# Turning the memory queries on VectorE and through DRAM in place of TensorE transposes, in a two-layer hybrid decoder

## The chip, the cores and the metric

The kernel runs on one core of one Trainium2 chip. The metric is the device time of one execution in microseconds (us); the runs of the kernel before took 383.99, 384.08 and 385.17 us, median 384.08. The profile is of one further execution, taken by the hardware profiler.

Engines are called TensorE (PE; its weight loads are PEld), VectorE (DVE), ScalarE (ACT), GpSimd (POOL) and SyncE (SP, here only an issuer of DMAs). A line such as L1259 is a line of the kernel before.

## The reference

Two layers work on `x` of 256 tokens by 1024 columns. Each normalises `x`, multiplies it by one wide input matrix, runs three branches side by side and adds the gated, projected result to `x`.

```python
for l in range(DEPTH):                                   # DEPTH = 2
    h = rms_norm(x, norm_g[l])
    proj = h @ w_in[l]                                   # 1024 x 5120
    q_a, k_a, v_a, q_h, f_h, i_h, q_m, z = jnp.split(proj, split_points, axis=-1)
    ...                                                  # o_a: causal attention, 8 heads x 64
    ...                                                  # o_h: HGRN2 recurrence, 4 heads x 128
    kv_m = rms_norm(mem, mem_norm_g[l]) @ w_mem_kv[l]    # 256 memory tokens
    k_m, v_m = jnp.split(kv_m, 2, axis=-1)
    km = rms_norm(k_m.reshape(B, M, MEM_HEADS, MEM_HEAD_DIM), mem_k_norm[l])
    qm = rms_norm(q_m.reshape(B, S, MEM_HEADS, MEM_HEAD_DIM), mem_q_norm[l])
    o_m = memory_attention(qm, km, vm).reshape(B, S, G)  # 4 heads x 128
    y = jnp.concatenate([o_a, o_h, o_m], axis=-1) * jax.nn.silu(z)
    x = x + y @ w_out[l]
```

The change is about `qm`, the queries of the memory branch: 256 tokens by 512 columns (4 heads of 128).

## The kernel before

**Weights in chunks.** All weights pass through SBUF as 60 chunks per layer, each 128 rows by 1024 columns (512 KB). SyncE loads a chunk into `wr` (4 buffers), ScalarE casts it to a rounded high half `wh` (3 buffers, line 213), and VectorE subtracts to get the low half `wl` (3 buffers, line 227). A product is three matmuls: high by high, high by low, low by high. Chunk numbers below count from a layer's start: 0 to 7 memory keys and values, 8 to 15 the HGRN forget and query gates, 16 to 19 keys, 20 to 23 HGRN input, 24 to 27 queries, 28 to 31 HGRN gate, 32 to 35 memory queries, 36 to 39 values, 40 to 43 and 44 to 47 the two other gates, 48 to 59 the output projection. A chunk of the values is 12 matmuls of 512 columns on PE (lines 292 to 294); a chunk of the gates is eight of 512 columns with `wh` and then eight of 256 columns with `wl` (line 275).

**Side work.** All else of the branches is written as generators that are stepped between the matmul groups. A scheduler sets the order of each engine's instructions; where it is not left to it, `in_turn` chains (functions `order_of_attention`, `order_of_memory`) write the order out by hand: which `wl` stands ahead of which piece of VectorE's side work, and the same for ScalarE. Engines and queues work strictly in their order, so a piece that waits holds all that stands behind it.

**The memory queries.** `g_qm` (line 1241) copies the two PSUM results to `qm` on ScalarE, takes the sums of squares, and then turns `qm` so that the head dimension lies on the partitions: for each half `t` of the tokens, four TensorE transposes of 128x128 into a PSUM tile (line 1259), a ScalarE cast to the high half `qmh` (line 1261) and a VectorE subtraction to the low half `qml` (line 1262). That makes 8 transposes per layer and 16 in all. They are placed among the values' matmuls. `g_mem_unit` then multiplies `qmh` and `qml` with the turned keys (`kmh`, `kml`; 24 score matmuls of 256 columns per layer, printed as line 275 `sd<-kml,qmh` and so on), takes row maxima (`mxm`), a scaled negative maximum (`nbm`), exponentials on ScalarE (line 1300) and the rest of the softmax.

**The other way to turn a tile.** `across` (line 88) is used for keys, queries, the HGRN output and the attention weights P: VectorE transposes 32x32 blocks into a tile `blk` (line 95), one DMA writes it to DRAM (`there`, line 106), and four DMAs read it back in the turned order, 32 partitions each (line 111). The default queue is SyncE's; with `q=nc.gpsimd` all five DMAs are on GpSimd's. The tile `blk` is one buffer, unless `stage` names the tag of another.

## Time and profile before

| | |
|---|---|
| median of the runs (range) | 384.08 us (383.99 to 385.17) |
| the profiled execution | 383.72 us, span 381.9 us |
| PE busy | 376.4 us, 99% of the span |
| PEld busy | 317.1 us, 83% |
| VectorE busy | 322.4 us, 84% |
| ScalarE busy | 250.5 us, 66% |
| GpSimd busy | 112.3 us, 29% |
| granted PE clock | 0.999 of full speed |
| DMA | 87.64 MB, mean 229 GB/s |
| stretch 129 to 135 us (scores of layer 0) | VectorE busy 6.00 of 6.00 us, DMA share 0.85 |

The span is the time from the first to the last instruction of the profiled execution. In a timeline a row has the start, the time from the first start to the last end of the merged instructions, engine, line, operation, output tile <- input tiles, and a count; a bracket tells how long the engine was idle ahead of it and what released it. Matmuls are pipelined, so their rows overlap and the distance of two starts tells more than a duration. The last rows of an answer on one tile give the time from a DMA's issue to its landing.

### The profile page before, as it was taken

The numbers are of one execution on the slowest core, as the hardware profiler recorded it, in microseconds if no ns is written. First come the engines' busy times: TensorE is split into PE (matmuls) and PEld (weight loads), VectorE is DVE, ScalarE is ACT, GpSimd is POOL, SyncE is SP. The second block draws the span as 40 slices with busy tenths as digits, with TensorE's granted clock in tenths as the row PEclk, the third lists the DMA queues.
The fourth block names the chain that finished last, engine by engine and source line by source line (L and its number), as shares of the span: only waits on it lengthen the run. The fifth ranks groups of instructions, "written<-read, shape, count | busy, mean of one in ns | idle before, by whom it ended". The sixth has DMA issues, their size and how long they took to land.

```text
span 381.9 us, 6807 instructions
## 1 busy us (share of the span) xinstructions
PE 376.4 (99%) x2431; PEld 317.1 (83%) x2431; DVE 322.4 (84%) x596; ACT 250.5 (66%) x428; POOL 112.3 (29%) x199
## 2 busy tenths in 40 slices
PE   8999999999999999999999999999999999999996
PEld 5888888878887898888888888888888888888885
DVE  4789978999769999967597889899897799998573
ACT  5988866439669839664367857455665993894540
POOL 3176889500700722220021030030052042225000
PEclk9999999999999999999999999999999999999999
DMA  8986695377823889896459667736876168989712
GB/s 267 419 321 190 235 288 172 118 269 232 295 82 128 269 274 355 307 270 214 167 175 317 189 203 233 257 125 232 257 223 222 55 246 266 348 262 307 224 57 110
DMA packets 27250, 87.64 MB, mean 229 GB/s; under 512 B 3792, under 2 KB 6224, under 8 KB 27216
## 3 DMA queue, kind: packets, MB, share of 16 engines
q1 hardware_dynamic: 22304, 71.31, 55.0%
q0 software_dynamic: 4624, 15.73, 13.8%
q8 instruction: 19, 0.31, 0.3%
q10 hardware_dynamic: 288, 0.15, 0.1%
q14 instruction: 15, 0.12, 0.1%
HBM read 76.18 MB, written 11.01 MB: 228 GB/s over the span
## 4 chain that ended last, share of the span: by engine, by line
PE 76%; POOL 7%; DVE 7%; DMA 3%; issue 3%; ACT 2%; DVEq 0%; ACTq 0%
PE acc L275 19%; PE acc L1438 17%; PE acc L312 12%; PE acc L293 7%; PE acc L292 6%; PE acc L294 6%; PE sd L275 4%; PE sd L279 3%; DVE wl L227 2%; DMA qT<-there 1%; POOL rt L605 1%; POOL rt L606 1%; DMA there<-blk 1%; ACT P L1169 1%; POOL mk L653 1%
## 5 line engine op out<-in xcount | busy, mean ns | idle before, releaser
L227 DVE TENSOR_TENSOR wl<-wr,wh 128x1024 fp32r<-128x1024 f32 x96 | 116.7, 1219 | 17.7 <-ACT wh L213 17.5
L213 ACT CAST wh<-wr 128x1024 fp32r<-128x1024 f32 x96 | 100.9, 1053 | 46.0 <-PE acc L275 18.4
L293 PE MATMUL acc<-wl,hT 128*128 128x512 f32 x192 | 75.4, 393 | 0.3 <-DVE wl L227 0.3
L294 PE MATMUL acc<-wh,hT 128*128 128x512 f32 x192 | 74.8, 390 | 0.0
L292 PE MATMUL acc<-wh,hT 128*128 128x512 f32 x192 | 70.5, 395 | 0.0
L275 PE MATMUL acc<-hT,wh 128*128 128x512 f32 x256 | 64.0, 391 | 0.0
L275 PEld LDWEIGHTS acc<-hT,wh 128*128 128x128 f32 x256 | 46.4, 189 | 8.3
L292 PEld LDWEIGHTS acc<-wh,hT 128*128 128x128 f32 x192 | 35.9, 188 | 8.0 <-issue 0.7
L293 PEld LDWEIGHTS acc<-wl,hT 128*128 128x128 f32 x192 | 36.1, 188 | 7.6 <-DVE wl L227 0.5
L294 PEld LDWEIGHTS acc<-wh,hT 128*128 128x128 f32 x192 | 36.1, 188 | 7.5
L1438 PE MATMUL acc<-wl,yh 128*128 128x512 f32 (+1 forms) x96 | 37.1, 387 | 0.0
L1438 PE MATMUL acc<-wh,yl 128*128 128x512 f32 (+1 forms) x96 | 37.1, 387 | 0.0
L217 ACT ACTIVATE wh<-wr,gT 128x1024 fp32r<-128x1024 f32 (+1 forms) x29 | 28.6, 1002 | 12.4 <-DMA wr<-in_w_mem_kv_dram 4.8
L275 PEld LDWEIGHTS acc<-hT,wl 128*128 128x128 f32 x256 | 34.7, 190 | 2.2
L231 DVE SCALAR_TENSOR_TENSOR wl<-wr,gT,wh 128x1024 fp32r<-128x1024 f32 (+1 forms) x29 | 31.1, 1095 | 5.3 <-ACT wh L217 5.3
L275 PE MATMUL acc<-hT,wl 128*128 128x256 f32 x256 | 35.4, 282 | 0.0
L1438 PE MATMUL acc<-wh,yh 128*128 128x512 f32 (+1 forms) x96 | 30.6, 390 | 0.0
L106 POOL DMA_DIRECT2D there<-blk x9 | 5.8, 649 | 80.3 <-DVE hgm L699 39.8
L312 PE MATMUL acc<-wh,mTh 128*128 128x512 f32 x64 | 25.2, 396 | 0.4 <-ACT mTh L433 0.4
L312 PE MATMUL acc<-wh,mTl 128*128 128x512 f32 x64 | 24.8, 390 | 0.0
L1169 ACT ACTIVATE P<-P,nba,rq 128x128 f32<-128x128 f32 (+1 forms) x32 | 17.1, 544 | 8.0 <-DVE nba L1163 8.0
L1438 PEld LDWEIGHTS acc<-wh,yl 128*128 128x128 f32 x96 | 18.0, 188 | 3.7
(237 smaller groups left out, 648.8 us busy)
## 6 DMA issues: line engine op xcount, KB each, us to landing
wr<-in_w_in_dram SPq DMA_DIRECT2D x80, 512.0 KB, 4.4
wr<-in_w_out_dram SPq DMA_DIRECT2D x24, 512.0 KB, 7.3
wr<-in_w_mem_kv_dram SPq DMA_DIRECT2D x15, 512.0 KB, 5.2
there<-blk POOLq DMA_DIRECT2D x9, 512.0 KB, 5.0
there<-blk POOLq DMA_DIRECT2D x4, 768.0 KB, 6.2
PT<-there POOLq DMA_DIRECT2D x16, 192.0 KB, 5.8
there<-blk SPq DMA_DIRECT2D x4, 512.0 KB, 2.9
P<-there POOLq DMA_DIRECT2D x16, 128.0 KB, 7.3
```

Of the source, the lines that this page charges most:

```text
L213: N["wh", i] = nc.scalar.copy(whs[i], raws[i])
L217: N["wh", i] = nc.scalar.activation(whs[i][:, sl], raws[i][:, sl], AF.Copy, scale=gT[:, g:g + 1])
L227: N["wl", i] = nc.vector.tensor_tensor(wls[i], raws[i], whs[i].bitcast(F32), op=OP.subtract)
L231: ins = nc.vector.scalar_tensor_tensor(wls[i][:, sl], in0=raws[i][:, sl], scalar=gT[:, g:g + 1], in1=whs[i][:, sl].bitcast(F32), op0=OP.mu ...
L275: nc.tensor.matmul(o, lhsT=a, rhs=b, start=s, stop=e)
L279: ins = nc.tensor.matmul(o, lhsT=a, rhs=b, start=s, stop=e)
L292: N["mm", i, j, t] = nc.tensor.matmul(acc[t], lhsT=th[:, k, ts], rhs=wH, start=k == 0, stop=False)
L293: N["mm l", i, j, t] = nc.tensor.matmul(acc[t], lhsT=th[:, k, ts], rhs=wL, start=False, stop=False)
L294: N["mm r", i, j, t] = nc.tensor.matmul(acc[t], lhsT=tl[:, k, ts], rhs=wH, start=False, stop=k == 7)
L312: N["kv", i, g, t, j] = nc.tensor.matmul(acc[g][t], lhsT=x[:, c, ts], rhs=y, start=c == 0 and j == 0, stop=c == 7 and j == 2)
L1169: N["exp", u, c] = nc.scalar.activation(P[:, i, kc[t]], P[:, i, kc[t]], AF.Exp, bias=nb[:, c:c + 1], scale=rq[:, r:r + 1], accum_out=sm[:, ...
L1438: ins = nc.tensor.matmul(a, lhsT=y, rhs=wt[:, cs], start=n == (0 if to is None else nk - 2) and j == 0, stop=n == nk - 1 and j == 2)
```

## The change

`g_qm` no longer uses TensorE. Once the HGRN recurrence has used its input `ih` (new flag `recurred`), `qm` as a whole goes through `across`: one VectorE block transpose of 128x1024 into the space of `ih`, a write to DRAM on GpSimd's queue, and four loads back into `qm` on SyncE's queue (the new argument `back`). ScalarE then casts `qmh` and VectorE subtracts `qml` from SBUF, in the strided order that `across` leaves. In the hand-written order the block transpose stands behind `wl` 38 and ahead of the first P transpose (`turned0`), both `qml` stand ahead of `wl` 41 (before: one behind `wl` 39, one behind the HGRN output's transpose), both `qmh` stand behind the second `va` copy and ahead of `wh` 43, and the row maxima `mxm` of the scores, of which two were placed ahead of `wl` 42 and `wl` 43, are all behind `wl` 43.

```diff
-    def across(dst, src, n, stage=None, free=None, name=None, q=None, behind=None, pace=(2, 4)):
+    def across(dst, src, n, stage=None, free=None, name=None, q=None, behind=None, pace=(2, 4), back=None):
...
-            ins = q.dma_start(dst[c * 32:c * 32 + 32], there[:, :, c].rearrange("q j r -> j q r"))
+            ins = (back or q).dma_start(dst[c * 32:c * 32 + 32], there[:, :, c].rearrange("q j r -> j q r"))
...
+        done.add(f"recurred{l}")
         r = rsq("hg", ss, 8, 128)
...
-        yield 2
+        flat = qm.rearrange("p t s -> p (t s)")
+        while f"recurred{l}" not in done:
+            yield
+        yield from across(flat.rearrange("p (q r) -> p q r", q=4), flat, 8, "ih", q=nc.gpsimd, name=f"qm{l}", pace=(1, 1),
+                          back=nc.sync)
         qmh = sb.tile([128, 4, 256], F32R, name="qmh", tag="ih", bufs=1)
         qml = sb.tile([128, 4, 256], F32R, name="qml", tag="hF", bufs=1)
         for t in range(2):
-            ts = slice(t * 128, (t + 1) * 128)
-            yield from room("sd")
-            pt = side_tile()
-            for h in range(4):
-                N["qm turn", t, h] = nc.tensor.transpose(pt[:, h * 128:(h + 1) * 128], qm[:, t, h * 128:(h + 1) * 128],
-                                                         ident)
-            N["qmh", t] = nc.scalar.copy(qmh[:, :, ts], heads(pt, 4))
-            N["qml", t] = nc.vector.tensor_tensor(qml[:, :, ts], heads(pt, 4), qmh[:, :, ts].bitcast(F32), op=OP.subtract)
-            rel()
-        yield 2
+            N["qmh", t] = nc.scalar.copy(strip_of(qmh, t), strips(flat)[:, :, t])
+            N["qml", t] = nc.vector.tensor_tensor(strip_of(qml, t), strips(flat)[:, :, t],
+                                                  strip_of(qmh, t).bitcast(F32), op=OP.subtract)
+        yield
...
-        in_turn(w("wl", 37), w("wl", 38), ("across", f"turned0{l}"))
-        for h in range(4):
-            in_turn(("mm", c + 37, 1, 1), ("qm turn", 1, h))
+        in_turn(w("wl", 37), w("wl", 38), ("across", f"qm{l}"))
...
```

VectorE in layer 0, from `wl` of chunk 37 (`wl_1494`) over chunk 38 to chunk 39 (`wl_1593` before, `wl_1597` now); `P_1349` is the first P tile, `hgm` and `ssq` are small sums for the norms. Before:

```order
L227 TENSOR_TENSOR wl_1494<-wr_1359,wh_1445 128x1024
L227 TENSOR_TENSOR wl_1544<-wr_1384,wh_1492 128x1024
L95 STREAM_TRANSPOSE blk_1635<-P_1349 128x1536
L699 TENSOR_SCALAR hgm_1522<-ssh_1449 128x8
L695 TENSOR_REDUCE ssq_1550<-sq_1554 128x4
L695 TENSOR_REDUCE ssq_1550<-sq_1557 128x4
L227 TENSOR_TENSOR wl_1593<-wr_1443,wh_1542 128x1024
```

Now:

```order
L227 TENSOR_TENSOR wl_1494<-wr_1359,wh_1445 128x1024
L227 TENSOR_TENSOR wl_1544<-wr_1384,wh_1492 128x1024
L95 STREAM_TRANSPOSE blk_1566<-qm_1551 128x1024
L95 STREAM_TRANSPOSE blk_1625<-P_1349 128x1536
L699 TENSOR_SCALAR hgm_1522<-ssh_1449 128x8
L695 TENSOR_REDUCE ssq_1550<-sq_1554 128x4
L695 TENSOR_REDUCE ssq_1550<-sq_1557 128x4
L227 TENSOR_TENSOR wl_1597<-wr_1443,wh_1542 128x1024
```

The transpose of `qm` stands between `wl` 38 and the P transpose; all behind it, `wl` 39 with it, keeps its order.

TensorE in layer 0, from the last matmul of the values; `acc` are the gate group's results, `sd` those of the scores. Before:

```order
L294 MATMUL acc<-wh,hT 128x512
L275 MATMUL sd<-kml,qmh 128x256
L275 MATMUL sd<-kmh,qml 128x256
L275 MATMUL sd<-kmh,qmh 128x256
L275 MATMUL sd<-kml,qmh 128x256
L275 MATMUL sd<-kmh,qml 128x256
L275 MATMUL sd<-kmh,qmh 128x256
L275 MATMUL acc<-hT,wh 128x512 x7
```

Now:

```order
L294 MATMUL acc<-wh,hT 128x512
L275 MATMUL acc<-hT,wh 128x512 x24
L275 MATMUL acc<-hT,wl 128x256 x5
L275 MATMUL sd<-kml,qmh 128x256
L275 MATMUL acc<-hT,wl 128x256
L275 MATMUL sd<-kml,qmh 128x256 x3
L275 MATMUL acc<-hT,wl 128x256 x2
L275 MATMUL acc<-hT,wh 128x512 x6
L275 MATMUL sd<-kmh,qml 128x256
```

The first score matmul has moved behind the high-half matmuls of chunks 40 to 42 and five of the low-half ones of chunk 40; the 24 score matmuls themselves are the same.

More of the change, by code (lines that the diff above doesn't have):

```diff
@@ L1380, in order_of_attention @@
                 in_turn("score", (p, c + 34, t // 2, t % 2))
-        in_turn(w("wl", 37), w("wl", 38), ("across", f"turned0{l}"))
-        for h in range(4):
-            in_turn(("mm", c + 37, 1, 1), ("qm turn", 1, h))
+        in_turn(w("wl", 37), w("wl", 38), ("across", f"qm{l}"))
         in_turn(("last mask", 0), ("nba", 0), ("first mask", 1), ("last mask", 1), ("nba", 1), w("wl", 36), ("ria", 0),
                 *(("scale", 0, i) for i in range(5)), ("ss", "h", 0), *(("scale", 0, i) for i in range(5, 8)),
-                ("ss", "h", 1), w("wl", 37), ("across", f"turned0{l}"), ("ms", "hg"), ("ss", "qm", 0),
-                ("ss", "qm", 1), w("wl", 39), ("qml", 0), ("ms", "qm"), *(("zh", i) for i in range(8)), ("ria", 1),
-                w("wl", 40), ("across", f"zh{l}"), ("qml", 1), *(("scale", 1, i) for i in range(8)), w("wl", 41),
-                ("across", f"turned1{l}"), ("mxm", 0, 0), w("wl", 42), ("mxm", 1, 0), w("wl", 43))
+                ("ss", "h", 1), w("wl", 37), ("across", f"qm{l}"), ("across", f"turned0{l}"), ("ms", "hg"), ("ss", "qm", 0),
+                ("ss", "qm", 1), w("wl", 39), ("ms", "qm"), *(("zh", i) for i in range(8)), ("ria", 1),
+                w("wl", 40), ("across", f"zh{l}"), *(("scale", 1, i) for i in range(8)), ("qml", 0), ("qml", 1),
+                w("wl", 41), ("across", f"turned1{l}"), w("wl", 42), w("wl", 43))
         in_turn(*(("exp", 0, i) for i in range(5)), w("wh", 36), *(("exp", 0, i) for i in range(5, 8)),
                 ("sq", "h", 0), ("sq", "h", 1), w("wh", 37), ("qm", 0), ("sq", "qm", 0), w("wh", 38), ("qm", 1),
-                ("sq", "qm", 1), w("wh", 39), ("qmh", 0), *(("exp", 1, i) for i in range(8)), w("wh", 40), ("qmh", 1),
-                w("wh", 41), ("va", 0), w("wh", 42), ("va", 1), w("wh", 43))
+                ("sq", "qm", 1), w("wh", 39), *(("exp", 1, i) for i in range(8)), w("wh", 40),
+                w("wh", 41), ("va", 0), w("wh", 42), ("va", 1), ("qmh", 0), ("qmh", 1), w("wh", 43))
     def order_of_norm(l):
@@ L1415, in order_of_memory @@
         unit = lambda k, u: [(k, u, i) for i in range(4)]
-        in_turn(w("wl", 43), ("sum", A_, 0), ("mxm", 0, 1), ("mxm", 1, 1), w("wl", 44), ("sum", A_, 1), ("nbm", 0),
+        in_turn(w("wl", 43), ("mxm", 0, 0), ("mxm", 0, 1), ("sum", A_, 0), w("wl", 44), ("mxm", 1, 0), ("mxm", 1, 1), ("sum", A_, 1), ("nbm", 0),
                 w("wl", 45), ("sum", A_, 2), ("nbm", 1), w("wl", 46), ("rim", 0), *unit("scalem", 0), ("sum", A_, 3),
```

## The prediction

> **What bounds the kernel now.** I read the page first, then the timelines of TensorE (PE) and VectorE (DVE) where the transposes stand, then the DMAs' landing times.
>
> ```profile
> PE 376.4 (99%) x2431; PEld 317.1 (83%) x2431; DVE 322.4 (84%) x596; ACT 250.5 (66%) x428; POOL 112.3 (29%) x199
> ```
>
> PE is busy for 99% of the span of 381.9 us. So the kernel is one queue of matmuls: an instruction taken out of it is a gain of its own step in the queue, and a wait put into it is a loss of its length, unless something later absorbs either. The question is what PE has in the place of the 16 transposes.
>
> **What the transposes hold.** Here is PE around the eight of layer 0 (line 1259, two groups of four), down to the first matmul that needs the low half `wl` of chunk 39.
>
> ```profile
> 119.81 0.60 PE L1259 MATMUL sd<-ident,qm 128*128 128x128 f32 x4
> 120.70 0.50 PE L293 MATMUL acc<-wl,hT 128*128 128x512 f32 x1 [0.28 <-DVE wl L227]
> 121.03 0.39 PE L294 MATMUL acc<-wh,hT 128*128 128x512 f32 x1
> ...
> 122.62 0.60 PE L1259 MATMUL sd<-ident,qm 128*128 128x128 f32 x4
> 122.98 0.49 PE L293 MATMUL acc<-wl,hT 128*128 128x512 f32 x1
> 123.30 0.39 PE L294 MATMUL acc<-wh,hT 128*128 128x512 f32 x1
> ...
> 126.75 0.39 PE L293 MATMUL acc<-wl,hT 128*128 128x512 f32 x1
> 126.97 0.39 PE L294 MATMUL acc<-wh,hT 128*128 128x512 f32 x1
> ```
>
> Matmuls overlap, so the step is from start to start: 0.22 to 0.23 us for a plain one (126.75 to 126.97). From the second group's start to the second matmul behind it there are 0.68 us (122.62 to 123.30); without the transposes one plain step of 0.23 would stand there. A group holds PE for 0.45 us, not for its busy time. The first group is different. Behind it PE still waits 0.28 us for `wl` of chunk 37. With those transposes gone PE waits longer, and the matmul starts at 120.70 as before: gain 0.
>
> In layer 1 the same place, from the second matmul behind the first group:
>
> ```profile
> 306.30 0.39 PE L294 MATMUL acc<-wh,hT 128*128 128x512 f32 x1
> ...
> 312.03 0.39 PE L293 MATMUL acc<-wl,hT 128*128 128x512 f32 x1
> 312.25 0.39 PE L294 MATMUL acc<-wh,hT 128*128 128x512 f32 x1
> ```
>
> **What VectorE has just then.** VectorE's rows at the same place, layer 0 and then layer 1:
>
> ```profile
> 119.43 2.35 DVE L227 TENSOR_TENSOR wl<-wr,wh 128x1024 fp32r<-128x1024 f32 x2
> 121.70 1.77 DVE L95 STREAM_TRANSPOSE blk<-P 128x1536 f32<-128x1536 f32 x1
> ...
> 124.62 1.22 DVE L227 TENSOR_TENSOR wl<-wr,wh 128x1024 fp32r<-128x1024 f32 x1
> ...
> 129.70 1.24 DVE L95 STREAM_TRANSPOSE blk<-zh 128x1024 f32<-128x1024 f32 x1
> 130.86 0.66 DVE L1262 TENSOR_TENSOR qml<-sd,qmh 128x512 fp32r<-128x512 f32 x1
> ```
>
> ```profile
> 304.57 2.35 DVE L227 TENSOR_TENSOR wl<-wr,wh 128x1024 fp32r<-128x1024 f32 x2
> ...
> 309.76 1.24 DVE L227 TENSOR_TENSOR wl<-wr,wh 128x1024 fp32r<-128x1024 f32 x1
> ```
>
> The first row of each is `wl` of chunks 37 and 38, the wl behind it that of chunk 39. VectorE has no gap between them. Chunk 39 is ready at 125.84 in layer 0, and PE asks for it at 126.75: 0.91 us to spare. In layer 1 it is ready at 311.00 and wanted at 312.03: 1.03 us.
>
> **The change, part by part.**
>
> 1. Transposes out. Layer 0: 0 for the first group and 0.45 for the second. Layer 1, first group: `wl` of chunk 37 ends at 304.57 plus 1.22 (the duration of one), so 305.79; PE starts 0.05 behind such an end (120.65 and 120.70 in layer 0) and has its second matmul 0.33 later (120.70 to 121.03, after a wait), at 306.17 instead of 306.30: 0.13 gained. Second group 0.45 again. So PE comes to chunk 39 at 126.30 in layer 0 and at 312.03 - 0.58 = 311.45 in layer 1.
>
> 2. The new block transpose on VectorE. The order puts it right ahead of the P transpose, between `wl` 38 and `wl` 39. The row of that shape is the one of zh: the next instruction starts 1.16 us behind it (129.70 to 130.86). The P transpose is not held by a buffer: the new one writes into the space of `ih`, not of `blk`. `wl` 39 is then ready at 125.84 + 1.16 = 127.00, and PE's second matmul on it starts at 127.00 + 0.05 + 0.33 = 127.38, against 126.97 before: 0.41 us later. Layer 1: 311.00 + 1.16 + 0.38 = 312.54 against 312.25: 0.29 later. What was slack of about 1 us becomes a wait of about 0.75, and the gain is spent on it. This is the step on which the forecast rests.
>
> 3. The way through DRAM, ahead of the first score matmul.
>
> ```profile
> DMA to landing us min/median/max: 4.6/4.6/4.6
> L111 SPq DMA_DIRECT2D kT<-there x8: 302/423/434, 82.5 to 268.8; - x8
> DMA to landing us min/median/max: 2.8/2.9/5.4
> 129.01 0.28 PE L275 MATMUL sd<-kml,qmh 128*128 128x256 f32 x1
> L1125 ACT COPY qTs<-qT x4: 610/617/621, 103.9 to 288.4; 128x512 f32<-128x512 f32 x4
> ```
>
> The first row is the write that GpSimd issues at this place in layer 0 now, the next two are the keys' loads, which have the same shape and the same queue; then the first score matmul of PE, and a ScalarE cast of the queries' shape. The block transpose ends at 121.70 + 1.24 = 122.94, the write lands 4.6 later at about 127.5, SyncE issues four loads 0.42 apart, the last at 128.8, and the last lands at 131.7 (median) to 134.2 (longest). Then come two ScalarE casts at 0.62. By the order PE now has 24 plain matmuls on `wh` 40 to 42 and five short ones on `wl` 40 before its first score: from 129.42 (the values' matmuls end at 129.01 now, plus 0.41) it needs 24 x 0.225 = 5.4 and comes there at 134.8 at the earliest, 135.4 with the short ones at half a plain step (an estimate from their 256 columns). The first cast is done at 132.4 to 134.9. PE doesn't wait for it. Cost taken: 0.
>
> By the Trainium skill, "DMA: Bandwidth & Descriptors", section on the anatomy of one DMA, a GpSimd-issued transfer takes about 2.0 us plus its bytes at 436 GB/s, an estimate of 3.2 us for 512 KB. The trace disagrees here (4.6). By the page's figure the queries would land 1.4 us sooner and the slower rival below would lose nearly all its chance; the sum would stay.
>
> 4. What is queued behind the new waits. The rows for it: VectorE, then ScalarE's first exponential and PE's second half of the output projection's start, then ScalarE's weight cast.
>
> ```profile
> 131.43 1.91 DVE L1177 TENSOR_SCALAR P<-P,ria 128x128 f32<-128x128 f32 x8
> 133.25 1.22 DVE L227 TENSOR_TENSOR wl<-wr,wh 128x1024 fp32r<-128x1024 f32 x1
> ...
> 142.51 0.16 DVE L1293 TENSOR_TENSOR nbm<-mxm,nrm 128x4 f32<-128x4 f32 x1
> ...
> 155.39 0.75 DVE L363 TENSOR_TENSOR as<-acc,al 128x256 f32<-128x256 f32 x2
> ```
>
> ```profile
> 143.49 0.57 ACT L1300 ACTIVATE P<-sd,nbm,qmr 128x256 f32<-128x256 f32 x1
> 156.95 1.07 PE L1438 MATMUL acc<-wh,yh 128*128 128x512 f32 x4
> L213 ACT CAST wh<-wr 128x1024 fp32r<-128x1024 f32 x96 | 100.9, 1053 | 46.0 <-PE acc L275 18.4
> ```
>
> On SyncE's queue the four loads stand between the weights of chunks 42 and 43, so weight 43 is issued at about 129.2, not at 125.9 when `wl` 39 frees its buffer. On ScalarE the cast of chunk 43 (1.05) stands behind the two query casts, so it is done at 134.1 to 136.5, and PE asks for it eight short steps behind the first score, at about 136.3: covered but for 0.2 at the late end. On GpSimd one more issue precedes the P write; the power for the HGRN norm behind it meets a VectorE that is 1.16 later too. On VectorE both `qml` now stand ahead of `wl` 41, so `wl` 41, the softmax maxima, the exponentials and the sums of the gate group slip together.
>
> With the queries there by 132.7 the two `qml` start when the P scaling ends (about 133.4) and `wl` 41 starts at about 134.7, 1.45 late. VectorE does the same work as before from there to nbm, so nbm is at 143.96 and the exponentials at about 144.1, 0.6 late. The last sums of the gate group are ready at 156.14 now and PE overwrites their PSUM from 156.95: 0.81, plus the 0.41 by which PE itself is late, 1.2 us of cover. That holds until the queries land at about 133.3, 4.5 us behind their last issue. Bounds per layer: 0 (landing at 2.9) to 1.1 (landing at 5.4: 0.9 here, 0.2 at chunk 43). I take 0.1 per layer, near the median row of the same loads, and the same in layer 1, whose margins at these places I have not worked out row by row.
>
> **Sum:** 0.41 + 0.29 + 2 x 0.1 = +0.9 us of span. The profiled execution took 383.72 us, 1.8 more than its span; the median of the three runs is 384.08, 0.36 above it. So the span becomes 382.8 and the time 384.08 + 0.9 = 385.0 us. About 0.3% (1.15 us) is the least that a measurement of this kernel can tell from no change.
>
> **The rivals.**
>
> Slower: the queries land late. The loads meet the weights, the P write and its loads. If the last one takes as long as the keys' longest (5.4), VectorE stands at `qml` with `wl` 41 behind it, and the chain of item 4 ends at PE as a wait on the gate sums, with another at chunk 43. Price up to 1.1 per layer: 384.08 + 0.7 + 2.2 = 387.0; halfway 385.9. It decides from 4.5 us behind the last issue. For it: 5.4 is in the row; against it: the median is 2.9. Chance 0.42.
>
> No change, on the lower side: VectorE takes the transpose in time, because PE comes to chunk 39 later than I work out or the pieces before `wl` 39 close up. Then only the gains stay, 0.45 + 0.58 = 1.0: 383.1 us. For it: the two sides are only 0.75 apart. Against it: VectorE has no idle time there to give. Chance 0.08.
>
> Faster: all four groups pay their 0.45, 1.8 us: 382.3 us. That needs `wl` 37 in time for 119.81 as well as `wl` 39 for 126.3, and `wl` 37 ends at 120.65 with nothing in the change that moves it. Chance 0.06.
>
> A rule against my sum's price: the Trainium skill, "VectorE: DVE Perf Modes", section on the three transpose paths, gives VectorE 311 ns for a 128x128 (2-byte type), an estimate of 2.5 us for the eight, and its rules for kernel authors keep a 128x128 transpose on TensorE. By it `wl` 39 would come 1.3 us later in each layer and the time would be about 387.4. The zh row (1.24 us for that shape) says no; I leave it no chance of its own.
>
> **How the numbers follow.** The forecast (a short wait for `wl` 39, queries in time) has 0.44 and is within 0.3%, the lower no-change case 0.08, slower 0.42, faster 0.06. Some of the forecast's own spread (0.1 more per layer in two places) crosses the bound, and some of the slower rival stays below it; these I let cancel. The range reaches from the lower no-change case to the full price of the slower one: 383.1 to 387.0.
>
> **What would show it.** Right: PE's waits hold two of about 0.75 us for `wl` on line 293, at chunk 39 of each layer, and the last wl of the values' stretch ends about 1.2 us later than before, behind two block transposes in a row. The queries' loads land less than 4.5 us behind the last issue, and PE doesn't wait from the scores to the output projection. Wrong to the slow side: ScalarE waits for the queries past 133.3, or PE for the sums of line 363. Wrong to the fast side: no wait of PE at chunk 39.

## The result and the profile after

| | before | after |
|---|---|---|
| median (range) of four runs each | 384.03 us (383.84 to 385.17) | 387.5 us (387.1 to 390.51) |
| ratio, 95% interval | | 1.0106 (1.0079 to 1.0133) |

The change made the kernel slower by 3.5 us. The forecast was 385.0 with a range up to 387.0, so the result lies 0.5 above the range. The changed kernel was timed twice more among the experiments below, beside the kernel before on the same chip each time: 1.0041 (0.9993 to 1.0089) and 1.0099 (1.0075 to 1.0124). Ratios leave disturbed executions out, so they are not quite the quotients of the medians.

The execution of the changed kernel that was profiled with the result took 390.51 us, 3 more than the others. The profile of the third group (`g_after3`, 387.91 us) is the typical one, and all rows "after" are from it. First its engines and TensorE's waits: what waits, for what, us in total, times, longest.

```profile
PE 376.8 (98%) x2415; PEld 315.0 (82%) x2415; DVE 325.5 (84%) x598; ACT 251.1 (65%) x428; POOL 112.2 (29%) x201
```

```profile
PE acc L293 <- DVE wl L227: 1.4, 3, 0.6
PE acc L275 <- ACT wh L213: 1.4, 2, 0.8
...
PE sd L279 <- DMA PT<-there: 0.8, 1, 0.8
...
PE acc L1435 <- DVE as L363: 0.2, 1, 0.2
```

The first row is chunk 37 of layer 0 as before and, new, chunk 39 of each layer. The other three rows did not exist before: the high half of chunk 43, the turned attention weights, the gate sums. Where they stand:

```profile
126.78 0.50 PE L293 MATMUL acc<-wl,hT 128*128 128x512 f32 x1 [0.54 <-DVE wl L227]
...
137.03 1.21 PE L275 MATMUL acc<-hT,wh 128*128 128x512 f32 x4 [0.84 <-ACT wh L213]
...
313.38 0.50 PE L293 MATMUL acc<-wl,hT 128*128 128x512 f32 x1 [0.56 <-DVE wl L227]
...
323.37 0.98 PE L275 MATMUL acc<-hT,wh 128*128 128x512 f32 x3 [0.57 <-ACT wh L213]
...
344.95 1.20 PE L1435 MATMUL acc<-wh,yh 128*128 128x512 f32 x4 [0.25 <-DVE as L363]
...
350.27 1.57 PE L279 MATMUL sd<-PT,va 128*64 128x256 f32 x16 [0.80 <-DMA PT<-there]
```

Waits alone don't give the sum: behind the wait at 126.78 the next matmul starts 0.33 us later, where a plain step is 0.23. So I measured from start to start on TensorE, between four places that both kernels have: A, the last pair of line 275 `sd<-ih,hX` (the recurrence); C, the first matmul of the output projection (`acc<-wh,yh`); M, the first `sd<-mP,vmh` of layer 1; and the last matmul. These rows carry layer 1, before and then after:

```profile
299.47 0.39 PE L275 MATMUL sd<-ih,hX 128*128 128x128 f32 x2
...
339.49 1.09 PE L1438 MATMUL acc<-wh,yh 128*128 128x512 f32 x4
```

```profile
300.70 0.39 PE L275 MATMUL sd<-ih,hX 128*128 128x128 f32 x2
...
341.79 1.09 PE L1435 MATMUL acc<-wh,yh 128*128 128x512 f32 x4
...
362.80 0.28 PE L279 MATMUL sd<-mP,vmh 128*128 128x256 f32 x1
```

| stretch on TensorE, us | before | after | difference |
|---|---|---|---|
| start to A, layer 0 | 113.66 | 113.85 | +0.19 |
| A to C, layer 0 | 40.54 | 41.60 | +1.06 |
| C of layer 0 to A of layer 1 | 145.27 | 145.25 | -0.02 |
| A to C, layer 1 | 40.02 | 41.09 | +1.07 |
| C to M, layer 1 | 19.37 | 21.01 | +1.64 |
| M to the last matmul | 19.18 | 19.42 | +0.24 |

The sum is +4.18, and the two profiled executions differ by 387.91 - 383.72 = 4.19. So there are two losses: one of about 1.1 per layer where the change was made, and one of 1.9 from the output projection of layer 1 on. Both vary from execution to execution. Of the two other profiles of the changed kernel, that of 390.51 us has waits of 1.39 and 0.32 for chunk 43 and a stretch from C to M 2.27 above before; in `g_after_again` (388.32) they are 0, 0.39 and 0.13. The stretch from the start to A, ahead of everything that was changed, takes 113.5 to 116.9 us over the profiles of this case, which is spread of the kernel and not of the change.

**The first loss: weight 43.** What stands on SyncE's queue at this place, before and after, with the ScalarE and VectorE rows that follow in the kernel after:

```profile
125.86 4.27 SPq L177 DMA_DIRECT2D wr<-in_w_in_dram  x2
```

```profile
129.05 1.98 SPq L111 DMA_DIRECT2D qm<-there  x4
131.13 0.85 SPq L177 DMA_DIRECT2D wr<-in_w_in_dram  x2
...
133.46 1.14 ACT L1260 CAST qmh<-qm 128x512 fp32r<-128x512 f32 x2 [2.55 <-DMA qm<-there]
...
134.11 1.29 DVE L1261 TENSOR_TENSOR qml<-qm,qmh 128x512 fp32r<-128x512 f32 x2 [0.85 <-ACT qmh L1260]
...
135.94 1.04 ACT L213 CAST wh<-wr 128x1024 fp32r<-128x1024 f32 x1 [1.34 <-DMA wr<-in_w_in_dram]
```

Weight 43 was issued at 125.86 and is issued at 131.13, when the four loads are out. Those waited for the written tile, which GpSimd issued at 123.0. Landing times in the kernel after, of that write (layer 0, then layer 1) and of weight 43 (the same):

```profile
DMA to landing us min/median/max: 6.0/6.0/6.0
```

```profile
DMA to landing us min/median/max: 4.4/4.4/4.4
```

```profile
DMA to landing us min/median/max: 4.7/4.7/4.7
```

```profile
DMA to landing us min/median/max: 5.9/5.9/5.9
```

Weight 43 lands at 131.13 + 4.7 = 135.8, ScalarE waits 1.34 for it, its cast ends at 136.98, and TensorE had come to it at 137.03 - 0.84 = 136.19. In layer 1 it is issued at 316.29, lands at 322.2, and TensorE waits 0.57.

**The second loss: mostly GpSimd's chain.** GpSimd's queue carries four ways through DRAM one behind the other: P's first half (PT), the HGRN output (zh), P's second half (PT), and the memory weights (P). Each stands until its write has landed. Layer 1 before, then after:

```profile
324.89 2.22 POOL L111 DMA_DIRECT2D zh<-there  x4 [7.06 <-DMA there<-blk]
...
335.52 2.23 POOL L111 DMA_DIRECT2D PT<-there  x4 [7.78 <-DMA there<-blk]
...
346.13 2.24 POOL L1333 DMA_DIRECT2D P<-there  x4 [1.19 <-DMA there<-blk]
```

```profile
328.46 1.65 POOL L111 DMA_DIRECT2D zh<-there  x3 [8.60 <-DMA there<-blk]
...
340.06 2.24 POOL L111 DMA_DIRECT2D PT<-there  x4 [8.75 <-DMA there<-blk]
...
352.24 2.24 POOL L1332 DMA_DIRECT2D P<-there  x4 [3.80 <-DMA there<-blk]
```

Counted from A, the three loads start at 25.4, 36.1 and 46.7 us before and at 27.8, 39.4 and 51.5 after: each link adds to the lateness, and the last is 4.9 us late. The first link's loads (PT) are 0.8 late; after that the three written tiles that the chain waits for land 8.6, 8.9 and 9.5 us behind their issue, where it was 7.4, 7.9 and 7.6 before, which is 4.0 of the 4.9. TensorE's new wait for `PT<-there` belongs to the third link.

Matmul by matmul against the kernel before, the 1.88 is 0.49 at the gate sums (line 363), 1.09 at `PT<-there` and 0.30 at the memory branch's matmuls, which need P. The gate sums are not on GpSimd's chain. VectorE stood 0.53 us for ScalarE's `sg` there, and ahead of `sg` a cast of an output weight had waited for its landing:

```profile
340.44 1.15 ACT L217 ACTIVATE wh<-wr,gT 128x1024 fp32r<-128x1024 f32 x1 [1.03 <-DMA wr<-in_w_out_dram]
```

### The profile page after: what moved, and what is told of

Same layout as the page of the kernel before. It is cut to its first block, busy times and chain, and to the rows that moved or that the text cites. A ratio compares the mean times of both kernels' runs of the same rounds, so it can differ in the third digit from the quotient of the medians.

```text
span 388.7 us, 6802 instructions
## 1 busy us (share of the span) xinstructions
PE 377.4 (97%) x2415; PEld 315.5 (81%) x2415; DVE 325.4 (84%) x598; ACT 251.1 (65%) x428; POOL 112.2 (29%) x201
## 4 chain that ended last, share of the span: by engine, by line
PE 48%; DMA 14%; DVE 12%; issue 10%; POOL 9%; ACT 5%; SPq 1%; ACTq 0%; DVEq 0%; POOLq 0%
PE acc L1435 13%; PE acc L275 12%; PE acc L312 11%; DMA there<-blk 4%; DMA wr<-in_w_in_dram 3%; DMA wr<-in_w_out_dram 3%; DVE wl L227 3%; PE sd L275 3%; PE acc L293 3%; PE acc L292 2%; PE acc L294 2%; ACT wh L213 2%; DMA P<-there 2%; DMA qT<-there 2%; POOL rt L605 1%
## 5 line engine op out<-in xcount | busy, mean ns | idle before, releaser
L275 PEld LDWEIGHTS acc<-hT,wh 128*128 128x128 f32 x256 | 46.4, 188 | 10.7 <-ACT wh L213 2.1
L293 PEld LDWEIGHTS acc<-wl,hT 128*128 128x128 f32 x192 | 36.0, 188 | 11.5 <-DVE wl L227 4.4
L294 PEld LDWEIGHTS acc<-wh,hT 128*128 128x128 f32 x192 | 36.1, 188 | 7.4
L106 POOL DMA_DIRECT2D there<-blk x11 | 6.8, 619 | 82.1 <-DVE blk L95 77.1
L1435 PEld LDWEIGHTS acc<-wh,yh 128*128 128x128 f32 x96 | 17.7, 188 | 4.5 <-ACT yh L129 0.9
```

Source lines behind the costliest of these rows:

```text
L106: q.dma_start(there.rearrange("q j c r -> (q j) c r"), blk)
L275: nc.tensor.matmul(o, lhsT=a, rhs=b, start=s, stop=e)
L293: N["mm l", i, j, t] = nc.tensor.matmul(acc[t], lhsT=th[:, k, ts], rhs=wL, start=False, stop=False)
L294: N["mm r", i, j, t] = nc.tensor.matmul(acc[t], lhsT=tl[:, k, ts], rhs=wH, start=False, stop=k == 7)
L1435: ins = nc.tensor.matmul(a, lhsT=y, rhs=wt[:, cs], start=n == (0 if to is None else nk - 2) and j == 0, stop=n == nk - 1 and j == 2)
```

## The experiments

All were timed beside the kernel before on the same chip. Ratios are to that, with the 95% interval; the kernel before had medians of 383.64 to 385.87 and a wider spread there (383.2 to 388.6 over all groups) than with the result. Theory V says that VectorE's block transpose carries the loss, theory Q the standing of SyncE's queue, theory D the bytes.

| run | median, us | ratio (interval) |
|---|---|---|
| f_neither | 383.63 | 0.998 (0.9955 to 1.0006) |
| f_dve_only | 385.9 | 1.0048 (1.0013 to 1.0082) |
| f_dma_only | 390.18 | 1.0108 (1.0058 to 1.0157) |
| h_after43 | 388.77 | 1.0123 (1.0082 to 1.0164) |
| g_after_again | 388.97 | 1.0041 (0.9993 to 1.0089) |
| g_before_bytes | 385.71 | 0.9997 (0.9966 to 1.0027) |
| f_dma_quarter | 384.46 | 0.9966 (0.9932 to 1.0001) |
| h_behind39 | 400.29 | 1.0391 (1.0342 to 1.0439) |
| g_before_wait | 388.39 | 1.0107 (1.0074 to 1.0141) |
| g_bytes2 | 385.21 | 1.0009 (0.9978 to 1.0041) |
| h_gpsimd | 393.58 | 1.0207 (1.0164 to 1.025) |
| g_wait_only | 388.53 | 1.0105 (1.0068 to 1.0142) |
| g_bytes3 | 391.66 | 1.0186 (1.0135 to 1.0236) |
| g_before_wait2 | 389.79 | 1.0117 (1.0076 to 1.0157) |
| h_scalar | 391.6 | 1.018 (1.0137 to 1.0223) |
| g_after3 | 387.92 | 1.0099 (1.0075 to 1.0124) |
| g_wait_only2 | 386.38 | 1.0073 (1.0048 to 1.0098) |

### The change taken apart

**Neither part** (`f_neither`):

```diff
-        yield from across(flat.rearrange("p (q r) -> p q r", q=4), flat, 8, "ih", q=nc.gpsimd, name=f"qm{l}", pace=(1, 1),
-                          back=nc.sync)
+        yield 3
```

> This kernel has no turning of the queries at all: neither the 16 TensorE transposes nor VectorE's block transpose nor the way through DRAM (the queries are cast as they lie, so their channels are not turned). Theory Q (the loads of the queries stand on SyncE's queue ahead of weight 43, SyncE stands still until the written tile has landed, weight 43 comes late, and TensorE waits for its upper part; 1.39 and 0.32 us in the profile after) and theory V (VectorE's block transpose ahead of the lower part of weight 39 carries the loss) both give less than before by about the transposes that are gone: 382.5 to 383.5, with the wait of line 275 on wh 43 gone and that of line 293 on wl 39 gone. Theory C (the loss is in the rewritten order of the queries' casts and of the softmax's parts behind them, not in either piece) gives 385.5 or more.

**The block transpose alone** (`f_dve_only`):

```diff
+        blk = sb.tile([128, 4, 256], F32, name="blk", tag="ih", bufs=1)
+        N["across", f"qm{l}"] = nc.vector.transpose(blk.rearrange("p c (n i) -> p c n i", n=8),
+                                                    flat.rearrange("p (n c i) -> p c n i", n=8, c=4))
```

> VectorE's block transpose of the queries is made at its place ahead of the lower part of weight 39, its result is not used, and nothing is written to DRAM or loaded (the queries are cast as they lie). Theory V: the wait of line 293 on wl 39 stays at about 0.6 us in each layer, and most of the loss with it: 386.5 to 387.5. Theory Q: only that wait stays, about 2 times 0.6 us above the kernel with neither piece: 384 to 385, and no wait on wh 43.

**The way through DRAM alone** (`f_dma_only`):

```diff
+        N["across", f"qm{l}"] = nc.vector.tensor_scalar(one, one, 1.0, None, op0=OP.mult)
+        nc.gpsimd.dma_start(there.rearrange("q j c r -> (q j) c r"), flat.rearrange("p (c r) -> p c r", c=4))
+        for c in (0, 2, 1, 3):
+            nc.sync.dma_start(dst[c * 32:c * 32 + 32], there[:, :, c].rearrange("q j r -> j q r"))
```

> The way through DRAM alone: GpSimd's write and SyncE's four loads stand where they stand in the changed kernel, but what is written is the queries as they lie; VectorE makes one operation on 128x1 in place of the block transpose (the queries are not turned rightly). Theory Q: weight 43 still lands late and TensorE waits for wh 43 by 0.3 to 1.4 us in a layer: 386 to 387, no wait on wl 39. Theory V: like the kernel with neither piece, at most 384.

The kernel with neither part is no slower than before, so the rewritten order as such costs nothing that can be told. The block transpose alone gives 1.0048, 2.3 us above neither; the way alone 1.0108. Theory V, which wanted nearly the whole loss in the first and none in the second, falls as the only cause; each part has a price. In layer 1, from A to the last `acc<-wl,hT` matmul of the values, TensorE needs 14.37 before, 13.76 with neither, 14.64 with the block transpose and 13.76 with the way alone. So the transposes' removal is worth 0.61 there, the block transpose costs 0.88, and the net is 0.27. From A to C it is 40.02, 39.40, 40.22 and 40.34: the way costs 0.94. The two prices add up there: 0.82 and 0.94, against 1.69 for the changed kernel (41.09 - 39.40). TensorE's waits in the run with the way alone:

```profile
PE acc L275 <- ACT wh L213: 3.2, 2, 2.9
```

It is the wait for chunk 43 again, with no wait for chunk 39. (This profile, 391.84 us, is one of the slower executions of the six; what the wait of 2.86 did to the clock stands in the last section.)

**A quarter of the bytes** (`f_dma_quarter`), the transfers and places of the run before it:

```diff
-        nc.gpsimd.dma_start(there.rearrange("q j c r -> (q j) c r"), flat.rearrange("p (c r) -> p c r", c=4))
+        nc.gpsimd.dma_start(there.rearrange("q j c r -> (q j) c r")[:, 0], flat[:, 0:256])
...
-            nc.sync.dma_start(dst[c * 32:c * 32 + 32], there[:, :, c].rearrange("q j r -> j q r"))
+            nc.sync.dma_start(dst[c * 32:c * 32 + 32, 0], there[c, :, 0])
```

> The way through DRAM alone, as in the run with the way and no block transpose, with the same transfers in the same places and a quarter of the bytes: 128 KB written and four times 32 KB loaded per layer, and the loads still wait on SyncE for the written tile (queries not turned rightly, and three quarters of them not moved). Theory D: a quarter of the loss, 384 to 385. Theory Q: SyncE still stands until the write has landed, weight 43 is still late: 386 or more. Theory V: 384 or less.

0.9966: the loss is gone, against theory Q as it stood. With 128 KB the write lands 1.6 us sooner, SyncE's loads come at 127.12, 13.3 behind A, where the full size has them at 130.17, 14.9 behind, and three quarters of the bytes are gone. This run can't tell which of the two saves it; the kernels further below were made for that.

### Where the loads stand

**Behind weight 43** (`h_after43`):

```diff
-            ins = (back or q).dma_start(dst[c * 32:c * 32 + 32], there[:, :, c].rearrange("q j r -> j q r"))
+            with tc.issue_after(T["load", past].ins) if past is not None else nullcontext():
+                ins = (back or q).dma_start(dst[c * 32:c * 32 + 32], there[:, :, c].rearrange("q j r -> j q r"))
```

> The changed kernel with the four loads of the queries behind weight 43 on SyncE's queue in place of ahead of it. Theory Q: weight 43 is issued some 6 us earlier, no wait on wh 43 is left, and the time falls to 384.5 to 385.5; the queries are loaded at nearly the same time, since SyncE waits for the written tile either way. Theory V: 387.5, as the changed kernel. If the queries are what is late, their casts come later and the waits on the softmax's sums and on the later weight grow: 388 or more.

It gained nothing, 1.0123. TensorE's waits for `wh` fell to 0.6 us in total, but ScalarE now stands for the next weights:

```profile
138.36 1.05 ACT L218 CAST wh<-wr 128x1024 fp32r<-128x1024 f32 x1 [1.52 <-DMA wr<-in_w_in_dram]
...
145.27 1.06 ACT L218 CAST wh<-wr 128x1024 fp32r<-128x1024 f32 x1 [1.78 <-DMA wr<-in_w_in_dram]
```

The lateness moved from chunk 43 to the chunks behind it.

**On GpSimd's queue** (`h_gpsimd`; `back=nc.gpsimd` in place of `back=nc.sync`) **and on ScalarE's** (`h_scalar`; `back=nc.scalar`):

> The changed kernel with the four loads of the queries on GpSimd's queue, where their write stands, so that SyncE goes on with the weights. Theory Q: the wait on wh 43 goes, and in layer 1 the stretch from the last product of the recurrence to the first of the mixed output, 40.85 us in the profile after, comes to 40.2, as in the kernel with the block transpose alone; a ratio of about 1.003 to before, if GpSimd's next work (the factors of the queries' norm and the loads of the transposed probabilities) still has cover. Theory V: the ratio of the changed kernel, 1.004 to 1.012. If GpSimd's work has no cover, waits on PT or on the softmax's exponentials take the place of the one removed.

> The changed kernel with the four loads of the queries on ScalarE's queue, behind the upper part of weight 40, where they stand at 129 to 131 us and the written tile has landed or is about to; SyncE goes on with the weights. Price of its own: four issues of about 0.43 us ahead of the upper part of weight 41. Theory Q for the changed kernel (most of its loss is the standing of SyncE's queue): at least half of the loss beside it goes, a ratio of 1.002 to 1.006. Theory D (the bytes and GpSimd's chain of ways through DRAM would be late anyway): the ratio of the changed kernel, within 0.3 per cent.

Both are worse than the changed kernel, 1.0207 and 1.018. On GpSimd the queries come late, and TensorE stands 2.75 us at the first score of layer 0:

```profile
134.18 2.28 POOL L111 DMA_DIRECT2D qm<-there  x4 [2.87 <-ACT va L823]
...
142.90 1.31 PE L275 MATMUL sd<-kml,qmh 128*128 128x256 f32 x3 [2.75 <-ACT qmh L1260]
```

This profile is of the longest of its executions (398.33 us; the others took 389.9 to 394.1), so the size of the wait need not be typical. On ScalarE four issues take 2.33 us of its time ahead of the cast of chunk 41, and a string of waits follows:

```profile
128.18 2.33 ACTq L111 DMA_DIRECT2D qm<-there  x4
131.72 0.50 PE L275 MATMUL acc<-hT,wh 128*128 128x512 f32 x1 [0.23 <-ACT wh L213]
...
137.25 1.03 PE L275 MATMUL sd<-kml,qmh 128*128 128x256 f32 x3 [0.62 <-ACT qmh L1260]
```

So these two runs can't say what SyncE's standing is worth in the changed kernel: what was removed there was paid for elsewhere. Tried were three other places, and none was cheap.

**The block transpose behind `wl` 39** (`h_behind39`):

```diff
-                ("ss", "h", 1), w("wl", 37), ("across", f"qm{l}"), ("across", f"turned0{l}"), ("ms", "hg"), ("ss", "qm", 0),
-                ("ss", "qm", 1), w("wl", 39), ("ms", "qm"), ...
+                ("ss", "h", 1), w("wl", 37), ("across", f"turned0{l}"), ("ms", "hg"), ("ss", "qm", 0),
+                ("ss", "qm", 1), w("wl", 39), ("across", f"qm{l}"), ("ms", "qm"), ...
```

> The changed kernel with VectorE's block transpose of the queries behind the lower part of weight 39 in place of ahead of it, so that the written tile and the loads come about 1.2 us later. Theory V: the waits of 0.58 us on wl 39 go, 386 to 387, at least 1 us less than the changed kernel beside it. Theories D and Q: the bytes and the wait on SyncE's queue stay and come later, no gain or up to 1 us more, 388 to 389.

1.0391, 14 us slower. The expectation had the delay wrong: between the two places lie P's block transpose and the queries' sums, and in layer 1 the two writes, P's and the queries', leave GpSimd from 13.1 us behind A, where the changed kernel has them at 9.0 and 10.7. TensorE's waits:

```profile
PE sd L275 <- ACT qmh L1260: 4.3, 2, 2.2
PE acc L275 <- ACT wh L213: 3.2, 4, 1.9
```

The wait for `wl` 39 did go (13.79 from A to the last `wl` matmul of the values, as with neither part), but the queries' loads start 16.2 us behind A in place of 13.4, and from A to C layer 1 takes 46.10 against 41.09 of the changed kernel: 2.8 us on the queries' way cost 5.0. The casts of the weights stand behind the queries' casts on ScalarE, so one late transfer holds up what follows.

### The way beside the unchanged kernel before

These kernels keep the 16 TensorE transposes and the order of TensorE and VectorE (`g_bytes3` moves two matmuls among their neighbours) and add transfers whose data nobody uses.

**Both the bytes and the wait** (`g_before_wait`, and again as `g_before_wait2`):

```diff
+        there = away.tile([4, 32, 4, 256], F32, name="there", tag="there", bufs=5)
+        nc.gpsimd.dma_start(there.rearrange("q j c r -> (q j) c r"), qm.rearrange("p t s -> p (t s)").rearrange("p (c r) -> p c r", c=4))
...
+            nc.sync.dma_start(dst[c * 32:c * 32 + 32], there[:, :, c].rearrange("q j r -> j q r"))
```

> The kernel before with everything that it has (16 TensorE transposes, the order of TensorE, VectorE and ScalarE) and beside it the way through DRAM as the changed kernel has it: GpSimd writes the 512 KB of the queries' tile, and SyncE loads four pieces of 128 KB of the written tile back into it, about weight 43, when TensorE has read it. No engine uses what is loaded; only SyncE waits for the write. Theory Q, now with the size in it (SyncE stands until the written tile has landed, which takes 6 us for 512 KB and less for a quarter): weights 43 and 44 are issued 4 to 6 us late, TensorE waits for wh 43, 0.3 to 1.4 us in a layer: a ratio of 1.002 to 1.007. Theory V: no change.

> The run with the wait and the 1.05 MB again, beside the two that hold one of them each on the same chip. All theories: 1.007 to 1.014, as at the first time.

**Bytes without a wait**: `g_before_bytes` (the residual written, pieces of an input loaded), `g_bytes2` (512 KB written, 256 KB loaded) and `g_bytes3` (768 KB written, 256 KB loaded). The core of the last:

```diff
+        for c in (0, 2, 0):
+            if c == 0:
+                there = away.tile([4, 32, 4, 256], F32, name="there", tag="there", bufs=5)
+            nc.gpsimd.dma_start(there.rearrange("q j c r -> (q j) c r")[:, c:c + 2],
+                                qm[:, 1].rearrange("p (c r) -> p c r", c=2))
...
+            nc.sync.dma_start(qm[c * 32:c * 32 + 32, 0].rearrange("p (q r) -> p q r", q=2),
+                              dram(x, c * 16384, [[256, 32], [8192, 2], [1, 256]]))
```

> The kernel before, with its 16 TensorE transposes and the order of TensorE and VectorE as they were, and beside it transfers that nobody waits for: GpSimd writes 512 KB to DRAM per layer (of the residual), and SyncE loads four pieces of 128 KB from an input into the queries' tile after TensorE has read it. Nothing on SyncE waits for a landing. Theory D (the DMA engines are full from 132 to 144 us, shares 1.00, 1.01 and 1.02 in the profile after, and the 1.05 MB more per layer push weights 43 to 46 back, wherever their issue stands): 386 to 388. Theory Q (SyncE's wait for the written tile holds up the weights behind it) and theory V (VectorE's block transpose): 384, as before, by at most 0.5 more.

> As the run beside it, but nothing on SyncE waits: GpSimd writes 512 KB (the first half of the queries' tile, twice) and SyncE loads four pieces of 64 KB from an input into the other half, about weight 43. The earlier run of this kind had its write issued at 93 us, 30 us ahead of the place, so it tested the loaded bytes alone; this one reads the queries' tile and so can't be issued ahead of 121 us. Theory D (the bytes themselves, in the stretch in which the DMA engines are full): at least half of what the run with the wait costs, 1.002 or more. Theory Q: within 0.1 per cent of before, with no wait on wh 43.

> The kernel before with the full 1.05 MB per layer and no wait: GpSimd writes three times 256 KB from one half of the queries' tile, and cannot issue them before TensorE's transposes have their operand (120 to 124 us), and SyncE loads four pieces of 64 KB from an input into the other half, ahead of weight 43, without standing. Theory D (the bytes alone): 1.005 or more. Theory Q: 1.002 or less. Theory QD: 1.000 to 1.005, with GpSimd's last loads of the way (P) later by 2 to 4 us against TensorE, at the edge of what TensorE covers.

**A wait without bytes** (`g_wait_only`, and again as `g_wait_only2`):

```diff
+        if name is not None and name.startswith("zh"):
+            N["late", name] = nc.sync.dma_start(src[0:1, 0:8], dram(x, 0, [[8, 1], [1, 8]]))
...
+        in_turn(("late", f"zh{l}"), ("load", c + 43))
```

> The kernel before with a wait of SyncE's queue and no bytes: ahead of weight 43 SyncE loads 32 bytes into the tile that VectorE has just block-transposed (zh, which is loaded anew later), so that it stands until that transpose has ended, near 131 us in the profile before, and issues weight 43 about 5 us later than before, as late as in the changed kernel. Orders of all other engines as before. Theory Q (the standing of SyncE's queue alone): a ratio of 1.005 or more, with waits on wh 43. Theory QD (it takes both: the late weights and the 1.05 MB per layer, which together make the landings longer on GpSimd's chain of ways through DRAM): below 1.004, with the wait on wh at most a part.

> The kernel before with the wait of SyncE's queue and no bytes, again: its first profile fell on the one execution of six that was as fast as before (384.08, where the others took 388.1 and more), and shows no loss to explain. All theories: 1.007 to 1.014. If the profile falls on a typical execution, theory Q expects waits on wh 43 to 46 or, with the landings of the later ways through DRAM pushed back by the bunched weights, on PT and mP.

The way beside the kernel before costs 1.0107 and 1.0117, as much as the whole change. The wait alone costs 1.0105 and 1.0073, and the bytes alone between nothing (0.9997, 1.0009) and 1.0186, by their number and time: in `g_before_bytes` the write had gone out 30 us early, in `g_bytes2` it stood 4.6 us behind A, in `g_bytes3` three writes at 6.5, ahead of P's first write on GpSimd's queue. That P write was issued no later than before in `g_bytes3`, but it landed after 7.5 and 8.0 us in place of 4.6 and 4.9. So neither theory Q nor theory D holds alone: a wait without bytes is enough, the same total of bytes without a wait is enough in one of three forms, and the two don't add up. The waits are not of one size, either: weight 43 is issued 5.1 to 5.4 us late in the runs with the wait alone, and 1.3 to 3.8 late in the two with the way.

None of these profiles has a wait on `wh` 43 (A to C in layer 1 is 40.01 to 40.03, as before), although weight 43 is up to 5.4 us late. Most of the loss is on GpSimd's chain, at `PT` and `mP`. Two rows of `g_before_wait` and two of `g_wait_only2`, layer 1:

```profile
350.75 1.57 PE L279 MATMUL sd<-PT,va 128*64 128x256 f32 x16 [0.90 <-DMA PT<-there]
...
364.63 0.39 PE L279 MATMUL sd<-mP,vmh 128*128 128x256 f32 x1 [1.19 <-DVE mP L198]
```

```profile
351.48 2.24 POOL L1337 DMA_DIRECT2D P<-there  x4 [5.62 <-DMA there<-blk]
...
362.12 0.39 PE L283 MATMUL sd<-mP,vmh 128*128 128x256 f32 x1 [1.73 <-DVE mP L202]
```

In `g_before_wait2` and `g_bytes3` most of it falls in layer 0: from C to M there they take 24.47 and 23.88 us, against 19.37 before, for the same third link. One row of each:

```profile
165.58 2.73 PE L279 MATMUL sd<-PT,va 128*64 128x256 f32 x16 [2.95 <-DMA PT<-there]
```

```profile
163.93 2.38 PE L279 MATMUL sd<-PT,va 128*64 128x256 f32 x16 [2.19 <-DMA PT<-there]
```

Of these 5.1 and 4.5 us only 2.95 and 2.19 are the wait; most of the rest comes behind it, while the granted clock is down (last section). `g_wait_only2` loses a further 1.73 us behind M in the same way.

In layer 1 the time at which GpSimd starts its last loads (P), counted from C, is a mark of the chain's lateness, and it orders the runs:

| run | P's loads, us behind C | C to M, us | above before |
|---|---|---|---|
| before | 6.6 | 19.37 | |
| g_after_again | 8.5 | 19.50 | 0.13 |
| g_bytes2 | 8.6 | 19.38 | 0.01 |
| g_wait_only (384.08, the one execution of six without the loss) | 9.5 | 19.68 | 0.31 |
| g_before_bytes | 9.8 | 19.87 | 0.50 |
| g_before_wait2 | 10.1 | 20.04 | 0.67 |
| g_after3 | 10.5 | 21.01 | 1.64 |
| after (the execution of 390.51) | 11.1 | 21.64 | 2.27 |
| g_bytes3 | 11.2 | 21.49 | 2.12 |
| g_wait_only2 | 11.2 | 21.87 | 2.50 |
| g_before_wait | 11.5 | 21.95 | 2.58 |

Up to 2 us of lateness TensorE pays at most 0.13; at 3 to 3.5 us it pays 0.3 to 0.7, and at 4 to 5 us 1.6 to 2.6. So a small difference of bytes or of a place can decide whether there is a loss at all. That this is also why one kernel's executions spread by several us fits the two executions of `g_wait_only` and `g_wait_only2`, but was not followed through the other executions, which have no profile. (In the runs with the loads elsewhere, and in `f_neither` and `f_dma_only`, TensorE loses a further 1 us here to late `wl` of the output weights, with P's loads in time; they are not in the table.)

**The changed kernel again** (`g_after_again`, `g_after3`), two more rows of the table of all runs:

> The changed kernel itself, unchanged, beside the kernel before on the same chip as the other runs of this group. All theories: 387 to 389, a ratio near 1.01; its profile shows where TensorE stands late at each stage in an execution that is not the slowest of its runs.

> The changed kernel itself, beside the run with the loads on ScalarE's queue on the same chip: a ratio of 1.004 to 1.012 by all theories, as in the two earlier groups.

No version tried with the queries turned beats the kernel before, and the kernel with neither part, which only bounds what any of them could reach, is at 0.998.

## Why the prediction was wrong

**Item 1, the transposes: right.** 0.61 us in layer 1 by the run with neither part, 0.58 predicted. In layer 0, from the matmul that waits for chunk 37 to the last `wl` matmul of the values, the kernel before takes 7.86 us and the runs with neither part and with the way alone 7.41: 0.45, as predicted for the second group. The 0 for the first group fits too: after, as before, the matmul that waits for `wl` 37 starts 0.05 us behind its end (120.41 and 120.46).

**Item 2, the block transpose ahead of `wl` 39: right in both layers.** The waits read 0.54 and 0.56 in the profile, counted from the end of the matmul ahead; from the next plain step, as the prediction counted its 0.75, the first is 0.70. Net, in layer 1 from A to the last `wl` matmul of the values: 14.62 against 14.37, +0.25 (predicted +0.29). In layer 0, from the wait for chunk 37 to that matmul: 8.26 against 7.86, +0.40 (predicted +0.41). The rows are the two ends after, then the second end before; its first, 120.70, stands in the prediction:

```profile
120.46 0.50 PE L293 MATMUL acc<-wl,hT 128*128 128x512 f32 x1 [0.30 <-DVE wl L227]
...
128.72 0.39 PE L293 MATMUL acc<-wl,hT 128*128 128x512 f32 x1
```

```profile
128.56 0.39 PE L293 MATMUL acc<-wl,hT 128*128 128x512 f32 x1
```

Counted from A the two kernels look equal there (14.87 and 14.90), because the wait for chunk 37, which ends with a VectorE row, comes 0.43 us sooner behind A in this execution; over the profiles of this case it comes 6.6 to 8.0 us behind A, with and without the change. By the Trainium skill, "VectorE: DVE Perf Modes", section on the three transpose paths, eight 128x128 on VectorE are an estimate of 2.5 us. The trace has 1.24 for the instruction and 0.88 of loss for it, so that the 387.4 which the prediction had by that rule came out near the measured time is luck.

**Item 3, the way through DRAM: right in its cost of 0, wrong in the landing that it took.** TensorE did not wait for the first score. But the write landed after 6.0 us in layer 0, not 4.6, and the last load at 133.4, the latest time that the working allowed. By the Trainium skill, "DMA: Bandwidth & Descriptors", section on the anatomy of one DMA, it is an estimate of 3.2 us; the traces disagree, with 6.0 and 4.4 here and 6.5 in `f_dma_only`.

**Item 4, what is queued behind: the step that failed.** It had weight 43 issued at 129.2 and chunk 43 "covered but for 0.2 at the late end", 0.1 per layer taken. The weight was issued at 131.13, 1.9 later, of which 1.4 are the write's longer landing. And it took 4.7 more to land, a term that the working had left out: it took the two query casts as all that stands ahead of that cast. With the issue at 129.2, a landing of 4.7 and a cast of 1.04 would have ended at 134.9, ahead of TensorE's 136.19, so in layer 0 it took both. In layer 1 the weight is issued 15.6 us behind A, as early as the prediction had it for layer 0 (129.2 - 113.66 = 15.5), and there its landing alone, 5.9 us, makes it late. Measured from the last `wl` matmul of the values to C, the stretch grows from 25.65 to 26.47 in layer 1 and from 25.64 to 26.73 in layer 0: 0.82 and 1.09, together 1.9, where 0.2 was taken. The change also brings TensorE to chunk 43 earlier, 22.3 us behind A (136.19). In the kernel before the scores stand ahead of it; this row begins with the last matmul of chunk 42, so chunk 43 begins at 139.28, 25.6 behind A:

```profile
139.05 2.23 PE L275 MATMUL acc<-hT,wh 128*128 128x512 f32 x9
```

That fits the runs beside the kernel before, where the same late weight made TensorE wait for nothing at this place.

**What was not in the sum at all: GpSimd's chain.** The prediction's own test was that TensorE "doesn't wait from the scores to the output projection". What comes behind that, 1.64 + 0.24 = 1.9 us here, is 0.49 at the gate sums and else the chain's. The gate sums the prediction did follow, with 1.2 us of cover in layer 0 and layer 1 not worked out; it was in layer 1 that they came late, through the output weights. It did not follow the four ways through DRAM that share GpSimd's queue and the DMA engines with the new one.

**Its signs of being wrong.** Both signs to the slow side came true by little: ScalarE waited for the queries until 133.46 (133.3 was the bound), and TensorE waited 0.25 us for the sums of line 363.

**The slower rival** had the right sign, and of its two places chunk 43 was the right one. Its cause was not what happened: it wanted the last query load to land more than 4.5 us behind its issue, and it landed after 2.8 in layer 0 and 4.46 in layer 1; the 0.2 that it gave to chunk 43 was 1.09 and 0.82. That its price of 1.1 per layer is near the first loss is luck. The run with the block transpose behind `wl` 39 shows what late queries really cost: 4 to 5 us per layer (A to C 45.74 and 46.10, against 41.60 and 41.09), in layer 0 with a stretch at half the clock in it (last section).

What stays open is how the loss of the changed kernel on GpSimd's chain divides into bytes and waiting. Beside the kernel before each can be enough by itself, and the runs that took the wait from SyncE's queue in the changed kernel put it on a queue that could not bear it either.

## What to carry to other kernels

A load that waits for a write holds every later transfer of its queue for the whole landing (here weight 43, from 125.86 to 131.13): count what stands behind it up to its own landing and its cast, not only to its issue. A chain of ways through DRAM has a cover of its own far from the change; before another way is added, measure how late its last link may start (here 2 us cost next to nothing, 4 us 1.6) and not only whether the first consumer is in time. An instruction of 0.45 us per group on the bound engine can be cheaper than a transfer for which no place tried, on three queues, was free.

## What the runs showed of the hardware

A quarter of the bytes did not make the write much quicker. From the DMA view of `f_dma_only`, then of `f_dma_quarter` (KB each, median us to landing):

```profile
there<-qm POOLq DMA_DIRECT2D x1, 512.0 KB, 6.5
```

```profile
there<-qm POOLq DMA_DIRECT2D x1, 128.0 KB, 4.9
```

The moment can matter as much as the size: writes of 256 KB landed after 2.4 to 2.9 us in `g_bytes2`, where two went out 4.6 to 5.2 us behind A, and after 4.7 to 6.8 us in `g_bytes3`, where three went out 6.5 to 8.1 us behind it.

And in the profile of `f_dma_only`, behind TensorE's wait of 2.86 us, the granted clock fell; the columns behind the busy times are the clock, the DMA share and GB/s:

```profile
130.00:140.00 10.00, 7.14 (x37) 5.89 (x36) 8.53 (x15) 3.92 (x6) 2.87 (x5) 0.94 0.87 240
140.00:150.00 10.00, 10.00 (x54) 9.20 (x54) 5.52 (x9) 3.46 (x5) 2.77 (x5) 0.72 0.96 353
```

The same happened in five other executions. In each the clock is 0.50 for a few us, read in windows of 0.1 us:

| run | TensorE's wait, us (end) | clock at 0.50, us |
|---|---|---|
| g_before_wait2 | 2.95 (165.58) | 165.7 to 169.2 |
| f_dma_only | 2.86 (139.66) | 138.8 to 145.7 |
| h_gpsimd | 2.75 (142.90) | 142.9 to 146.4 |
| g_bytes3 | 2.19 (163.93) | 164.4 to 167.9 |
| h_behind39 | 2.15 (140.67) | 142.4 to 145.9 |
| g_wait_only2 | 1.73 (362.12) | 363.5 to 367.0 |
| h_behind39 | 2.17 (331.28) and 1.92 (351.50) | never |
| after, f_neither, g_after_again, h_behind39, h_gpsimd | 1.53 to 1.66 (122 to 125) | never |

At half the clock a matmul of 512 columns takes a step of 0.43 us in place of 0.23, as in two rows of `g_wait_only2`:

```profile
365.03 0.63 PE L1443 MATMUL acc<-wh,yh 128*128 128x512 f32 x1
365.45 0.63 PE L1443 MATMUL acc<-wl,yh 128*128 128x512 f32 x1
```

So 3.5 us at half the clock cost 1.6 to 1.7 us on top of the wait in `g_before_wait2`, `g_bytes3` and `g_wait_only2`. The clock stayed up at every wait of TensorE in this stretch up to 1.66 us and went down at six of eight between 1.73 and 2.95; the length alone doesn't decide, and what else does was not tried.
